# Attention on Trainium2: queries and keys projected as channels by tokens, rotated there, and stacked per head by way of DRAM

## The chip, the core and the metric

One core of a Trainium2 chip runs the whole network, in one launch. The metric is the time on the device of one execution, in microseconds (us): 2022.48 us before the change, the median of 3 runs (2022.04 to 2023.08).

The engines are TensorE (PE; the loading of its stationary operand is shown apart, as PEld), VectorE (DVE), ScalarE (ACT), GpSimd (POOL) and SyncE (SP), which here only issues DMAs. SBUF is the memory on the chip, with 128 partitions; TensorE writes to PSUM; DRAM is reached by DMA. 1024 tokens, 1024 channels, all in float32. A large product is done as three products of split operands (`mm3`): hi x hi, hi x lo and lo x hi, where hi is the value rounded to the type float32r and lo the rest.

## The reference

Two layers: attention, then an HGRN recurrence, each followed by an MLP. The change lies in the attention of the first layer.

```python
def sliding_window_attention(h, positions, w_qkv, b_qkv, sinks, w_o):
    qkv = h @ w_qkv + b_qkv                      # 1024 tokens, 16 query heads, 4 key and value heads, 64 channels a head
    q, k, v = ...
    cos, sin = rotary_tables(positions)
    q = apply_partial_rotary(q, cos, sin)        # rotates the first 16 of the 64 channels: pairs (i, i + 8)
    k = apply_partial_rotary(k, cos, sin)
    # blocks of 128 tokens, each with its own and the previous block as keys
    scores = einsum('bnqkgd,bnskd->bnkgqs', qb, kb) * HEAD_DIM ** -0.5
    scores = where(mask, scores, NEG_INF)        # causal, window of 128
    m = maximum(max(scores), sink); e = exp(scores - m)
    probs = e / (sum(e) + exp(sink - m))
    return einsum('bnkgqs,bnskd->bnqkgd', probs, vb).reshape(...) @ w_o
```

h is the input after an rmsnorm with a gain. The kernel multiplies by the gain first and by the token's factor 1/rms after the projection.

## The kernel before

**Order of the work.** The program first writes all operations into a list (`Schedule.add`), each with the engine or engines it may run on, a planned cost and what it reads and writes. `Schedule.order` then plays the list forward with the planned costs and latencies (a DMA load 4.2 us, a store 3.2 us), taking on each engine the ready operation of the lowest rank, and back for due times; the best of four such passes gives the order in which each engine's instructions are issued and the buffer of each tile. On the chip that order is fixed: each engine works through its own list, and an instruction that waits holds those behind it. SP's list holds all large DMAs, so a load that must wait for a store holds the weight loads behind it. Tiles come from pools of fixed size, `BUFS`: 60 "a" tiles and 18 "t" tiles of 128x512, 6 raw weight tiles "wr", 5 each of split ones "wh" and "wl", 8 PSUM banks ("p" and "q", 4 each).

**Attention.** Tokens go in two halves of 512 (four blocks of 128). `attention` runs `qkv(0)` alone, then `attend(0)` between `qkv(1)`, then `attend(1)` between `o_proj(0)`, then `o_proj(1)` between the first pieces of the MLP.

`qkv` has three groups of 512 columns: `cg` 0 holds keys and values (256 each), 1 and 2 the queries of two pairs of key heads. Each group runs over 8 slices of the input channels (`kt`), with one weight tile each, and four blocks: tokens are the stationary operand, the weights move, and PSUM holds 128 tokens by 512 columns. 12 products of 512 columns to a weight tile, 96 to a group.

`projected` takes a block of queries out of PSUM on VectorE (factor and bias in one operation) and rotates it there: tokens lie in the partitions, so the tables `trig` are 128x8 for a block, and a rotation is four small operations (`rope`). `keys_values` does the same for keys, turns them into channels by tokens with two transposes on TensorE, and fills for each of three overlapping spans of blocks (`K_SPANS`) the tiles `ks` (hi, in both halves of the partitions; the second copy is made by POOL) and `kl` (lo in one half, zero in the other).

`attend` turns the queries the same way, 16 transposes for each pair of key heads and half, and writes `stacks`: a tile for each head with hi in 64 partitions and lo in the other 64. The scores of a block are then two products a head, of the stack with `ks` and with `kl`. After them come the masks, the softmax (with the sink as one more column), transposes of the probabilities and the products with the values.

Of the kernel before, what the change touches and what calls it, by code (L numbers as in the profile page):

```python
# [10 lines left out]
F32 = mybir.dt.float32  # L11
# [6 lines left out]
P = 128  # L18
# [3 lines left out]
NH = 2  # L22
# [19 lines left out]
CH = 64  # L42
QB = 32
LEVELS = 5
HOMES = "aaaaaaaaaaaa"
K_SPANS = ((-1, 3), (2, 6), (5, 8))

# [36 lines left out]
class Buf:  # L84
# [7 lines left out]
    def keys(self, part):  # L92
        return set(self.writer) | set(self.readers) if part is None else {*part, None}
# [287 lines left out]
class Net:  # L381
# [751 lines left out]


    def rope_tables(self):
        shape = (P, NBLK, ROT // 2)
        pos = self.const((P, NBLK), I32)
        self.dma(pos, self.io["pos"], 4 * P * NBLK)
        posf = self.const((P, NBLK))
        self.op("DVE", self.nc.vector.tensor_copy, [posf], [pos], 100, posf, pos)  # L1140
        ang = self.const(shape)
        for j, f in enumerate(INV_FREQ):
            self.ts("DVE", ang[:, :, j], posf, f, None, ALU.mult, None, NBLK)
        self.trig = []
        for shift in (0.25, 0.0):
            turns, r = self.const(shape), self.const(shape)
            n = NBLK * ROT // 2
# [9 lines left out]
            self.trig.append(r)  # L1157

    def attention_constants(self):
# [3 lines left out]
        self.bias = []  # L1163
        for cg in range(3):
            b = self.a()
            self.dma(b, self.io["bqkv"][cg].partition_broadcast(P), 4 * P * TH)
            self.bias.append(b)
# [9 lines left out]
    def rope(self, x, heads, n):  # L1177
        half = ROT // 2
        v = x.rearrange("p (h d) -> p h d", d=HD)[:, :, :ROT].rearrange("p h (a r) -> p h a r", a=2)
        prod = []  # L1180
        for tab in self.trig:
            y = self.t(F32, (P, 8, 2, half))[:, :heads]
            tb = tab[:, n].unsqueeze(1).unsqueeze(1).to_broadcast([P, heads, 2, half])
            self.tt("any", y, v, tb, ALU.mult, heads * ROT)
            prod.append(y)
        yc, ys = prod
        self.tt("any", v[:, :, 0], yc[:, :, 0], ys[:, :, 1], ALU.subtract, heads * half)
        self.tt("any", v[:, :, 1], yc[:, :, 1], ys[:, :, 0], ALU.add, heads * half)

    def k_tiles(self, i):  # L1190
        if self.ks[i] is None:
            late = [] if i else [self.x[KT - 1][0]]
            self.ks[i] = [self.a(F32R) for _ in range(NG)]
            self.kl[i] = [self.t(F32R) for _ in range(NG)]
            for g, z in enumerate(self.kl[i]):
                _, o = self.rows(g)
                self.memset(z[o].bitcast(F32).only("o"), 0.0, "Pool", late)
            if K_SPANS[i][0] < 0:
                for z in self.ks[i] + self.kl[i]:
                    self.memset(z[:, :P].bitcast(F32).only(-1), 0.0, "Pool", late)  # L1200
        return self.ks[i], self.kl[i]

    def rows(self, g):
        lo, hi = slice(0, HD), slice(HD, P)
        return (hi, lo) if g % 2 else (lo, hi)

    def first_loads(self):

# [16 lines left out]

    def qkv(self, hf, h, r, ahead=()):

        blocks = range(hf * BPH, hf * BPH + BPH)
        for cg in range(3):
            ps = {n: self.psum() for n in blocks}  # L1230
            for kt in range(KT):
                self.s.lead = LEAD
                c = kt % 2 * TH
# [3 lines left out]
                w = self.weight_split(raw, engines=("DVE", "ACT") if start else ("ACT",), parts=start)  # L1237
                self.s.lead = 0
                hh, hl = h[kt]
                for n in blocks:  # L1240
                    tok = slice((n % BPH) * P, (n % BPH) * P + P)
                    hi = hh[:, tok].only(n // 2) if start else hh[:, tok]
                    self.mm3(ps[n], (hi, hl[:, tok]), w, kt == 0, kt == KT - 1)
                    if kt == KT - 1:
                        self.projected(cg, n, ps[n], r[:, n % BPH : n % BPH + 1])
                yield

    def projected(self, cg, n, ps, r):
        if cg == 0:
            self.keys_values(n, ps, r)  # L1250
        else:
            q = self.a()
            self.stt(q, ps, r, self.bias[cg], ALU.mult, ALU.add)
            self.rope(q, 8, n)
            self.q[n][cg - 1] = q

    def keys_values(self, n, ps, r):
        W = NG * HD
        k = self.t(F32, (P, W))
        self.stt(k, ps[:, :W], r, self.bias[0][:, :W], ALU.mult, ALU.add, W)  # L1260
        if n % 2 == 0:
            self.v.append(self.a(F32, (P, 2, W)))
        v = self.v[n // 2][:, n % 2].only(n)
        self.stt(v, ps[:, W:], r, self.bias[0][:, W:], ALU.mult, ALU.add, W)
# [5 lines left out]
        self.rope(k, NG, n)  # L1270
        pk = self.psum("q")[:, : 2 * P].rearrange("p (g s) -> p g s", g=2)
        for gp in range(2):
            self.transpose(pk[:, gp], k[:, gp * P : gp * P + P])
        for i, (first, end) in enumerate(K_SPANS):
            if not first <= n < end:
                continue
            ks, kl = self.k_tiles(i)
            c = slice((n - first) * P, (n - first) * P + P)
            for g in range(NG):
                r, o = self.rows(g)  # L1280
                src, dst = pk[r, g // 2], ks[g][r, c].only(n)
                self.copy(dst, src, P, more=HALF["ACT"])
                self.tt("DVE", kl[g][r, c].only(n), src, dst.bitcast(F32), ALU.subtract, P, HALF["DVE"])
                self.ts("Pool", ks[g][o, c].only(n), dst, 1.0, None, ALU.mult, None, P)

    def attend(self, hf, out):

        blocks = range(hf * BPH, hf * BPH + BPH)
        for gp in range(NG // 2):
            stacks = [[None] * 4 for _ in range(2)]  # L1290
            for j in range(4):
                pq = self.psum("q")
                for n in blocks:
                    c = slice((n % BPH) * P, (n % BPH) * P + P)
                    self.transpose(pq[:, c], self.q[n][gp][:, j * P : j * P + P])
                for e in range(2):
                    r, o = self.rows(e)
                    s = self.a(F32R)
                    self.act(s[r], pq[r], AF.Copy, scale=HD**-0.5, more=HALF["ACT"])
                    self.stt(s[o], pq[r], HD**-0.5, s[r].bitcast(F32), ALU.mult, ALU.subtract, more=HALF["DVE"])  # L1300
                    stacks[e][j] = s
            for e in range(2):
                g = 2 * gp + e
                for j in range(2):
# [75 lines left out]

    def attention(self, layer):
        self.v, self.dv, self.ks, self.kl = [], [], [None] * 3, [None] * 3
        self.q = [[None] * 2 for _ in range(NBLK)]
        out = [{}, {}]
        ahead = self.first_loads()
        h = [self.scaled(layer, 0)]
# [548 lines left out]
def layout(i):  # L1935
# [8 lines left out]
    heads = np.arange(D).reshape(2, 2, 4, HD).transpose(0, 2, 1, 3).ravel()  # L1944
    cols = np.concatenate([np.arange(D, D + 2 * NG * HD), heads])
    rows = [
        (4 * g + 2 * r + j) * HD + d for g in range(NG) for j in range(2) for r in range(2) for d in range(HD)
    ]
# [5 lines left out]
        "pos": f(i["positions"][0].reshape(NBLK, P).T),  # L1954
        "sinks": f(i["attn_sinks"][0]),
        "bqkv": f(bq[cols].reshape(3, TH)),
# [44 lines left out]
```

## Time and profile before

| | |
|---|---|
| median of 3 runs | 2022.48 us |
| profiled execution, its own time | 2021.7 us |
| its span | 2019.9 us |
| granted TensorE clock | 0.999 of full |
| TensorE busy | 2009.3 us (99%) |
| VectorE busy | 1844.6 us (91%) |
| ScalarE busy | 1312.5 us (65%) |
| POOL busy | 61.7 us (3%) |
| bytes read and written in DRAM | 394.57 MB, 100.14 MB |

Names in the profile are the program's, without numbers: `a<-q` is an operation that reads a PSUM tile "q" and writes an "a" tile, `d` is a tile in DRAM, `c` a constant. In a row of a group stand the shapes, the count, the busy time in us, the mean duration of one in ns, the engine's idle time just before them in us, and what ended it. In the timeline a row has the start, the length in us, engine, line, operation, names, shapes and how many instructions were merged. Nearly every operation is recorded by the same helper, so all rows have line 435. Ends of matmuls are modelled, so the time of one is longer than its step in a run of them.

### The profile page before, as it was taken

What the parts mean: (1) busy time and instruction counts of PE and PEld (TensorE: products, weight loads), DVE (VectorE), ACT (ScalarE), POOL (GpSimd) and SP (SyncE); (2) the same over time, 40 slices, a digit from 0 to 9 for tenths busy, and PEclk for the clock granted to TensorE, in tenths of its full rate; (3) what the DMA queues carried; (4) which work ended last, traced back from release to release, by engine and by line L of the source; (5) the groups of instructions that cost most, each with busy time, mean ns of one, the idle gap of its engine ahead of it and who ended that gap; (6) DMA issues with size and microseconds to landing.
All of it is one profiled execution on the core that took longest, in us unless ns stands there. A gap on an engine that the chain in (4) does not pass through costs nothing.

```text
span 2019.9 us, 39908 instructions
## 1 busy us (share of the span) xinstructions
PE 2009.3 (99%) x13788; PEld 1702.1 (84%) x13788; DVE 1844.6 (91%) x3802; ACT 1312.5 (65%) x2775; POOL 61.7 (3%) x152
## 2 busy tenths in 40 slices
PE   9999999999999999999999999999999999999998
PEld 7878788899998888888888888888889998888887
DVE  8899989899999979989999999999999999997985
ACT  7577977667676544657666666676767677544573
POOL 4020000000000000000000000000000000000000
PEclk9999999999999999999999999999999999999999
DMA  6212487778889987845878889999798888997812
GB/s 230 79 48 74 136 260 259 257 253 284 282 272 316 319 280 234 272 162 185 284 280 285 288 284 317 316 303 315 260 296 288 267 294 284 325 316 235 270 53 84
DMA packets 275418, 497.38 MB, mean 246 GB/s; under 512 B 30992, under 2 KB 36368, under 8 KB 275216
## 3 DMA queue, kind: packets, MB, share of 16 engines
q1 hardware_dynamic: 275072, 494.81, 73.1%
q8 instruction: 109, 1.79, 0.4%
q14 instruction: 93, 0.76, 0.1%
q10 hardware_dynamic: 144, 0.02, 0.0%
HBM read 394.57 MB, written 100.14 MB: 245 GB/s over the span
## 4 chain that ended last, share of the span: by engine, by line
PE 91%; DVE 6%; ACT 1%; issue 1%; DMA 1%; SPq 0%; DVEq 0%; ACTq 0%
PE p L435 50%; PE q L435 41%; DVE t L435 2%; DVE a L435 1%; DVE m L435 1%; DVE wl L435 1%; DMA a<-d 0%; ACT a L435 0%; ACT t L435 0%; SPq L435 0%; ACT wh L435 0%; DVE sm L435 0%; DMA a<-in_x 0%; ACT m L435 0%; DVEq L1975 0%
## 5 line engine op out<-in xcount | busy, mean ns | idle before, releaser
L435 PE MATMUL p<-a,wh 128*128 128x512 f32 (+1 forms) x2832 | 779.7, 360 | 0.0
L435 PE MATMUL q<-a,wh 128*128 128x512 f32 x2020 | 624.6, 390 | 0.2 <-ACT t L435 0.2
L435 PEld LDWEIGHTS p<-a,wh 128*128 128x128 f32 x2832 | 502.1, 189 | 78.4 <-issue 0.4
L435 PE MATMUL p<-a,wl 128*128 128x512 f32 (+1 forms) x1416 | 504.5, 359 | 0.6 <-DVE wl L435 0.6
L435 PEld LDWEIGHTS q<-a,wh 128*128 128x128 f32 x2020 | 374.8, 188 | 74.2 <-ACT t L435 0.6
L435 PE MATMUL q<-a,wl 128*128 128x512 f32 x1008 | 391.3, 389 | 0.0
L435 ACT CAST wh<-m 128x512 fp32r<-128x512 f32 (+1 forms) x354 | 212.0, 605 | 208.7 <-PE q L435 100.9
L435 PEld LDWEIGHTS p<-a,wl 128*128 128x128 f32 x1416 | 266.0, 189 | 39.2 <-DVE wl L435 1.4
L435 ACT CAST wh<-wr 128x512 fp32r<-128x512 f32 (+1 forms) x324 | 194.4, 603 | 154.4 <-PE p L435 92.6
L435 DVE TENSOR_TENSOR wl<-m,wh 128x512 fp32r<-128x512 f32 (+1 forms) x354 | 235.4, 670 | 35.0 <-ACT wh L435 28.8
L435 DVE TENSOR_TENSOR wl<-wr,wh 128x512 fp32r<-128x512 f32 (+1 forms) x324 | 215.0, 668 | 20.9 <-ACT wh L435 19.7
L435 DVE TENSOR_TENSOR t<-t,t 128x512 f32<-128x512 f32 (+4 forms) x408 | 225.1, 576 | 7.2 <-ACT t L435 4.4
L435 DVE TENSOR_TENSOR a<-t,a 128x512 fp32r<-128x512 f32 (+2 forms) x321 | 211.1, 677 | 16.8 <-PE q L435 7.1
L435 PEld LDWEIGHTS q<-a,wl 128*128 128x128 f32 x1008 | 189.3, 188 | 39.2
L435 ACT ACTIVATE t<-t 128x512 f32<-128x512 f32 x288 | 179.1, 631 | 53.2 <-DVE t L435 47.1
L435 ACT CAST a<-t 128x512 fp32r<-128x512 f32 (+1 forms) x241 | 142.8, 606 | 24.3 <-DVE t L435 9.2
L435 ACT COPY t<-q 128x512 f32<-128x512 f32 (+2 forms) x254 | 111.3, 442 | 32.1 <-PE q L435 23.0
L435 DVE TENSOR_TENSOR t<-t,p 128x256 f32<-128x256 f32 x288 | 116.4, 417 | 15.9 <-PE p L435 11.9
L435 PE MATMUL p<-wh,a 128*128 128x512 f32 x384 | 124.7, 395 | 0.2
L435 DVE TENSOR_TENSOR m<-wr,wr 128x512 f32<-128x512 f32 (+1 forms) x184 | 119.7, 652 | 0.4
L435 DVE TENSOR_TENSOR a<-a,a 128x512 fp32r<-128x512 f32 (+2 forms) x151 | 100.8, 682 | 8.4 <-ACT a L435 4.7
L435 ACT CAST a<-a 128x512 fp32r<-128x512 f32 x136 | 82.5, 620 | 26.7 <-DVE a L435 21.1
(131 smaller groups left out, 2434.2 us busy)
## 6 DMA issues: line engine op xcount, KB each, us to landing
t<-d SPq DMA_DIRECT2D x592, 256.0 KB, 4.6
a<-d SPq DMA_DIRECT2D x318, 256.0 KB, 4.6
d<-t SPq DMA_DIRECT2D x290, 256.0 KB, 3.3
wr<-in_down SPq DMA_DIRECT2D x224, 256.0 KB, 4.2
wr<-in_up SPq DMA_DIRECT2D x172, 256.0 KB, 4.3
wr<-in_win SPq DMA_DIRECT2D x68, 256.0 KB, 5.2
d<-a SPq DMA_DIRECT2D x64, 256.0 KB, 3.4
wr<-in_wqkv SPq DMA_DIRECT2D x48, 256.0 KB, 2.8
```

The lines of the kernel that those rows point to most:

```text
L435: fn(*[place(a) for a in args], **{k: place(v) for k, v in kw.items()})
```

## The change

Queries and keys are now projected with the weights as the stationary operand and the 512 tokens of a half moving: PSUM holds 128 channels by 512 tokens. Values stay as they were, now as products of 256 columns. Columns of the weights are ordered so that the first of a group's tiles holds the rotated channels of its heads: the first of each pair in the upper 64 partitions, the second in the lower; the others hold channels that aren't rotated.

- `channels` multiplies by the token factor, spread over partitions (`shares`, from four products of 128x128 for each half), adds the bias (now one value to a partition) on ScalarE, and splits into hi and lo. A rotated tile is also copied with its halves exchanged (`other`, two ScalarE operations of 64 partitions) and combined with two tables on VectorE.
- `rope_tables` computes the angles in 128x64 (8 frequencies by 16 pieces of 64 tokens) and keeps cos, sin and -sin in DRAM; `table` loads each into 128x512 tiles by DMAs that repeat the 8 rows, once for keys and once for queries in each half.
- `rows_out` stores hi and lo in DRAM, in the order in which the heads need them: `dk` for keys, `dq` for each half and pair.
- `keys` loads `ks` and `kl` of each span from `dk`: `ks` by a source with a leading dimension of 2 and step 0. `kl` has its lo in the lower partitions' half for all heads.
- `attend` loads its 8 stacks of a pair from `dq`. All transposes of queries and keys are gone, and so are the three 128x512 bias tiles; the order of the coroutines and the pools are unchanged.

```diff
+    def table(self, hf, keys):
+        cos, sin = self.a(), self.a()
+        half, h = P // 2, ROT // 2
+        n = 2 * NG * h // 2 if keys else half
...
+        for z, k, d in ((cos, 0, 0), (cos, half, 0), (sin, 0, 2), (sin, half, 1)):
+            src = self.trig[d].rearrange("(i c) t -> i (c t)", i=h)[:, hf * TH : hf * TH + TH]
+            self.dma(z[k : k + n].only(k), src.unsqueeze(0).to_broadcast([n // h, h, TH]), 4 * n * TH)
+        return cos, sin
...
+    def channels(self, ps, r, bias, tables=None):
+        z, hi, lo = self.t(), self.t(F32R), self.t(F32R)
+        self.tt("DVE", z, ps, r, ALU.mult)
+        if tables is None:
+            self.act(hi, z, AF.Identity, bias=bias)
+            self.stt(lo, z, bias, hi.bitcast(F32), ALU.add, ALU.subtract)
+            return hi, lo
+        y, other = self.t(), self.t()
+        up, low = slice(0, P // 2), slice(P // 2, P)
+        self.act(y, z, AF.Identity, bias=bias)
+        for i, (a, b) in enumerate(((up, low), (low, up))):
+            self.act(other[b].only(i), z[a], AF.Identity, bias=bias[a], more=HALF["ACT"])
+        cos, sin = tables
+        self.tt("DVE", y, y, cos, ALU.mult)
+        self.tt("DVE", other, other, sin, ALU.mult)
+        self.tt("DVE", y, y, other, ALU.add)
+        self.copy(hi, y, TH, psum=False)
+        self.tt("DVE", lo, y, hi.bitcast(F32), ALU.subtract)
+        return hi, lo
+
+    def keys(self, hf, ps, r, tables):
+        q = P // 4
+        first = [(slice(i * q, i * q + q), d) for i, d in enumerate((0, ROT, ROT // 2, 3 * ROT // 2))]
+        bias = [self.bias[:, i : i + 1] for i in range(2)]
+        self.rows_out(self.dk, NG, self.channels(ps[0], r, bias[0], tables), first, hf)
+        self.rows_out(self.dk, NG, self.channels(ps[1], r, bias[1]), [(slice(0, P), 2 * ROT)], hf)
...
+        rows = self.dk.rearrange("(g s d) t -> g s d t", g=NG, s=2)
+        for i, (first, end) in enumerate(K_SPANS):
+            a, b = max(first, hf * BPH), min(end, hf * BPH + BPH)
...
+            for g in range(NG):
+                src = [rows[g, s][:, a * P : b * P].only(*read(s)) for s in range(2)]
+                self.dma(ks[g][:, c].bitcast(F32).only(*range(a, b)), src[0].unsqueeze(0).to_broadcast([2, HD, n]), 4 * P * n)
+                self.dma(kl[g][:HD, c].bitcast(F32).only(*range(a, b)), src[1], 4 * HD * n)
+
+    def rows_out(self, d, heads, parts, pieces, hf=None):
+        for s, z in enumerate(parts):
+            for rows, first in pieces:
+                n = rows.stop - rows.start
+                to = d.rearrange("(h s d) t -> h s d t", h=heads, s=2)[:, s, first : first + n // heads]
...
+                self.dma(to.only(...), z[rows].bitcast(F32), 4 * n * TH)
+
+    def queries(self, hf, gp, m, ps, r, tables):
+        half = P // 2
+        bias = self.bias[:, 2 + 4 * gp + m : 3 + 4 * gp + m]
+        parts = self.channels(ps, r, bias, None if m else tables)
+        pieces = [(slice(0, P), ROT * m)] if m else [(slice(0, half), 0), (slice(half, P), ROT // 2)]
+        self.rows_out(self.dq[hf, gp], NHQ // 2, parts, pieces)
...
     def qkv(self, hf, h, r, ahead=()):
-        blocks = range(hf * BPH, hf * BPH + BPH)
+        W = NG * HD
+        shares, tables = [self.a() for _ in range(2)], None
         for cg in range(3):
-            ps = {n: self.psum() for n in blocks}
+            if cg == 0:
+                kp, vp = ([self.psum() for _ in range(2)] for _ in range(2))
+            else:
+                qp = [self.psum() for _ in range(4)]
...
+                for b in range(BPH if cg == 0 else 0):
+                    tok = slice(b * P, b * P + P)
+                    hi = hh[:, tok].only(b // 2) if start else hh[:, tok]
+                    self.mm3(vp[b // 2][:, b % 2 * W : b % 2 * W + W], (hi, hl[:, tok]), tuple(z[:, W:] for z in w), ...)
+                for m, ps in enumerate(qp if cg else kp):
+                    self.mm3(ps, tuple(z[:, m * P : m * P + P] for z in w), (hh, hl), first, last)
                 yield
...
+            if cg == 0:
+                total = self.spread(r)
+                for z, scale in zip(shares, (1.0, HD**-0.5)):
+                    self.act(z, total, AF.Copy, scale=scale)
+                self.keys(hf, kp, shares[0], self.table(hf, True))
+                for b in range(BPH):
+                    self.value(hf * BPH + b, vp[b // 2][:, b % 2 * W : b % 2 * W + W], r[:, b : b + 1])
+                tables = self.table(hf, False)
+            else:
+                for m, ps in enumerate(qp):
+                    self.queries(hf, cg - 1, m, ps, shares[1], tables)
...
     def attend(self, hf, out):
         for gp in range(NG // 2):
-            stacks = [[None] * 4 for _ in range(2)]
-            for j in range(4):
-                pq = self.psum("q")
-                for n in blocks:
-                    c = slice((n % BPH) * P, (n % BPH) * P + P)
-                    self.transpose(pq[:, c], self.q[n][gp][:, j * P : j * P + P])
...
+            stacks = [[self.a(F32R) for _ in range(4)] for _ in range(2)]
+            for k, z in enumerate(sum(stacks, [])):
+                self.dma(z.bitcast(F32), self.dq[hf, gp][k * P : k * P + P], 4 * P * TH)
```

More of the change, by code (lines that the diff above doesn't have):

```diff
@@ L1157, in rope_tables @@
             self.trig.append(r)
+        minus = self.const((P, n))
+        self.ts("DVE", minus, self.trig[1], -1.0, None, ALU.mult, None, n)
+        kept = []
+        for z in (self.trig[0], self.trig[1], minus):
+            d = self.tile(f"d{self.n}", 1, (P, n), F32, self.dram)
+            self.dma(d, z, 4 * P * n)
+            kept.append(d)
+        self.trig = kept
+    def table(self, hf, keys):
+        cos, sin = self.a(), self.a()
+        half, h = P // 2, ROT // 2
+        n = 2 * NG * h // 2 if keys else half
+        if keys:
+            for k in (n, half + n):
+                self.memset(cos[k : k + n].only(f"o{k}"), 1.0, "Pool")
+                self.memset(sin[k : k + n].only(f"o{k}"), 0.0, "Pool")
+        for z, k, d in ((cos, 0, 0), (cos, half, 0), (sin, 0, 2), (sin, half, 1)):
+            src = self.trig[d].rearrange("(i c) t -> i (c t)", i=h)[:, hf * TH : hf * TH + TH]
+            self.dma(z[k : k + n].only(k), src.unsqueeze(0).to_broadcast([n // h, h, TH]), 4 * n * TH)
+        return cos, sin
     def attention_constants(self):
@@ L1162, in attention_constants @@
         self.dma(self.sink, self.io["sinks"].partition_broadcast(P), 4 * P * NHQ)
[L1163 to L1167, printed above, removed]
+        W = NG * HD
+        self.bias_v, self.bias = self.const((P, W)), self.const((P, 10))
+        self.dma(self.bias_v, self.io["bv"].partition_broadcast(P), 4 * P * W)
+        self.dma(self.bias, self.io["bqk"], 4 * P * 10)
+        self.ts("DVE", self.bias[:, 2:], self.bias[:, 2:], HD**-0.5, None, ALU.mult, None, 8)
         diff = self.t(I32, (P, P))
@@ L1175, in attention_constants @@
         self.memset(self.neg, NEG)
[L1177 to L1188, printed above, removed]
+        self.dk = self.tile(f"d{self.n}", 1, (2 * NG * HD, T), F32, self.dram)
@@ new lines, in attention_constants @@
+        self.dq = {(hf, gp): self.tile(f"d{self.n}", 1, (NHQ * HD, TH), F32, self.dram) for hf in range(NH) for gp in range(2)}
+    def channels(self, ps, r, bias, tables=None):
[17 more added lines that the diff above has]
+        return hi, lo
@@ new lines, in rows_out @@
+    def rows_out(self, d, heads, parts, pieces, hf=None):
[3 more added lines that the diff above has]
+                to = d.rearrange("(h s d) t -> h s d t", h=heads, s=2)[:, s, first : first + n // heads]
+                if hf is not None:
+                    to = to[:, :, hf * TH : hf * TH + TH]
+                self.dma(to.only(f"{'' if hf is None else hf}{s}{first}"), z[rows].bitcast(F32), 4 * n * TH)
+    def queries(self, hf, gp, m, ps, r, tables):
[4 more added lines that the diff above has]
+        self.rows_out(self.dq[hf, gp], NHQ // 2, parts, pieces)
@@ L1194, in k_tiles @@
             self.kl[i] = [self.t(F32R) for _ in range(NG)]
-            for g, z in enumerate(self.kl[i]):
-                _, o = self.rows(g)
-                self.memset(z[o].bitcast(F32).only("o"), 0.0, "Pool", late)
+            for z in self.kl[i]:
+                self.memset(z[HD:].bitcast(F32).only("o"), 0.0, "Pool", late)
             if K_SPANS[i][0] < 0:
-                for z in self.ks[i] + self.kl[i]:
+                for z in self.ks[i]:
                     self.memset(z[:, :P].bitcast(F32).only(-1), 0.0, "Pool", late)
+                for z in self.kl[i]:
+                    self.memset(z[:HD, :P].bitcast(F32).only(-1), 0.0, "Pool", late)
         return self.ks[i], self.kl[i]
-    def rows(self, g):
-        lo, hi = slice(0, HD), slice(HD, P)
-        return (hi, lo) if g % 2 else (lo, hi)
     def first_loads(self):
@@ L1239, in qkv, with value @@
                 hh, hl = h[kt]
-                for n in blocks:
[L1241 to L1245, printed above, removed]
-                yield
[L1248 to L1257, printed above, removed]
+                first, last = kt == 0, kt == KT - 1
+                for b in range(BPH if cg == 0 else 0):
+                    tok = slice(b * P, b * P + P)
+                    hi = hh[:, tok].only(b // 2) if start else hh[:, tok]
+                    self.mm3(vp[b // 2][:, b % 2 * W : b % 2 * W + W], (hi, hl[:, tok]), tuple(z[:, W:] for z in w), first and b % 2 == 0,
+                             last, W, skip_group_check=True)
+                for m, ps in enumerate(qp if cg else kp):
+                    self.mm3(ps, tuple(z[:, m * P : m * P + P] for z in w), (hh, hl), first, last)
+                yield
+            if cg == 0:
[9 more added lines that the diff above has]
+                    self.queries(hf, cg - 1, m, ps, shares[1], tables)
+    def value(self, n, ps, r):
         W = NG * HD
-        k = self.t(F32, (P, W))
-        self.stt(k, ps[:, :W], r, self.bias[0][:, :W], ALU.mult, ALU.add, W)
         if n % 2 == 0:
@@ L1269, in keys_values @@
             self.tt("any", self.dv[n // 2][:, n % 2].only(n), v, before, ALU.subtract, W)
[L1270 to L1284, printed above, removed]
     def attend(self, hf, out):
@@ L1943, in layout @@
     bq, wq = i["attn_b_qkv"][0], i["attn_w_qkv"][0]
-    heads = np.arange(D).reshape(2, 2, 4, HD).transpose(0, 2, 1, 3).ravel()
-    cols = np.concatenate([np.arange(D, D + 2 * NG * HD), heads])
+    head = lambda first, n, *dims: np.concatenate([np.add.outer(first + HD * np.arange(n), np.arange(*d)).ravel() for d in dims])
+    h = ROT // 2
+    keys = head(D, NG, (0, h), (ROT, ROT + h), (h, ROT), (ROT + h, 2 * ROT), (2 * ROT, HD))
+    queries = [head(gp * D // 2, NHQ // 2, (0, h), (h, ROT), *((k, k + ROT) for k in range(ROT, HD, ROT))) for gp in range(2)]
+    cols = np.concatenate([keys, np.arange(D + NG * HD, D + 2 * NG * HD), *queries])
     rows = [
@@ L1953, in layout @@
         "lb": f(col(lb)),
[L1954 removed]
+        "pos": f(np.broadcast_to(i["positions"][0].reshape(1, NCH, T // NCH), (ROT // 2, NCH, T // NCH)).reshape(P, T // NCH)),
         "sinks": f(i["attn_sinks"][0]),
[L1956 removed]
+        "bqk": f(bq[np.concatenate([keys, *queries])].reshape(10, P).T),
+        "bv": f(bq[D + NG * HD : D + 2 * NG * HD]),
         "wqkv": f(wq[:, cols].reshape(4, 2, P, 3, TH).transpose(3, 0, 2, 1, 4).reshape(3, 4, P, 2 * TH)),
```

40 lines of the change are left out of this document (22 added, 18 removed).

## The prediction

> **What bounds the kernel now.** I read the first part of the page (busy time of each engine), then the chain that ended last, then busy time in stretches of 25 us over the attention stage.
>
> ```profile
> span 2019.9 us, 39908 instructions
> PE 2009.3 (99%) x13788; PEld 1702.1 (84%) x13788; DVE 1844.6 (91%) x3802; ACT 1312.5 (65%) x2775; POOL 61.7 (3%) x152
> PE 91%; DVE 6%; ACT 1%; issue 1%; DMA 1%; SPq 0%; DVEq 0%; ACTq 0%
> 25.00:50.00 25.00, 25.00 (x116) 20.66 (x115) 23.95 (x65) 19.45 (x47) 14.72 (x24) 1.00 0.52 164
> 50.00:75.00 25.00, 25.00 (x151) 20.77 (x149) 19.64 (x55) 8.40 (x14) 2.10 (x4) 1.00 0.28 86
> 75.00:100.00 25.00, 25.00 (x137) 21.05 (x136) 23.63 (x61) 20.45 (x61) 1.96 (x6) 1.00 0.24 75
> 100.00:125.00 25.00, 24.79 (x145) 19.62 (x145) 21.17 (x66) 19.64 (x72) 10.63 (x21) 1.00 0.06 22
> ```
>
> The columns of a stretch are its length, then PE, PEld, DVE, ACT and POOL busy, the granted clock, the DMA share and GB/s. TensorE is the bound in every stretch and at full clock; VectorE is close behind it in the attention stage; the DMA engines are the only ones with room there. So a us of TensorE work taken out is a us gained, work on ScalarE, VectorE or POOL is worth almost nothing, and whatever makes TensorE wait is paid in full.
>
> **TensorE's own work.** The change takes out 80 transposes: 64 of queries (2 halves x 2 pairs of groups x 4 x 4 blocks) and 16 of keys. It adds two spreads of the norm factors over the partitions, 4 products of 128x128 each. The projections keep their count in columns; only the values' go from 512 columns to 256 (192 products instead of 96).
>
> ```profile
> L435 PE MATMUL q<-c,a 128*128 128x128 f32 x64 | 8.7, 274 | 0.0
> L435 PE MATMUL q<-c,t 128*128 128x128 f32 x16 | 2.8, 274 | 0.2 <-ACT a L435 0.2
> 73.25 1.97 PE L435 MATMUL q<-c,a 128*128 128x128 f32 x16
> L435 PE MATMUL q<-c,sm 128*128 128x128 f32 x32 | 4.4, 279 | 1.0 <-DVE sm L435 1.0
> 116.04 0.40 PE L435 MATMUL q<-a,a 128*128 128x256 f32 x2
> 116.27 0.40 PE L435 MATMUL q<-t,a 128*128 128x256 f32 x2
> 116.51 0.63 PE L435 MATMUL p<-wh,a 128*128 128x512 f32 x2
> 116.98 0.39 PE L435 MATMUL p<-wl,a 128*128 128x512 f32 x1
> 117.21 0.63 PE L435 MATMUL p<-wh,a 128*128 128x512 f32 x2
> ```
>
> The groups give 8.7 + 2.8 = 11.5 us, but the drain of the last product of each run is in that. Sixteen in a row took 1.97 us, 0.123 each: 80 x 0.123 = 9.8, the value I take. Spreads of the same form (two rows of the trace to a product) cost 4.4/32 = 0.14 a row, 16 rows: +2.2. Four products of 256 columns start within 0.47 us (0.1175 each), three of 512 within 0.70 (0.233): two short ones cost at most 0.005 more than a long one, 96 x 0.005 = +0.5. Sum on TensorE: -9.8 + 2.2 + 0.5 = **-7.1 us** (between -9.0 with 11.5 and -6).
>
> **ScalarE, VectorE and POOL.**
>
> ```profile
> L435 DVE SCALAR_TENSOR_TENSOR a<-q,a 64x512 fp32r<-64x512 f32 x32 | 21.8, 688 | 0.7
> L435 DVE TENSOR_TENSOR t<-q,a 64x128 fp32r<-64x128 f32 x40 | 11.5, 288 | 0.7
> L435 DVE SCALAR_TENSOR_TENSOR a<-p,sm,a 128x512 f32<-128x512 f32 x16 | 11.4, 744 | 2.0 <-PE p L435 2.0
> L435 DVE TENSOR_TENSOR t<-a,c 128x128 f32<-128x128 f32 x32 | 8.0, 282 | 0.0
> L435 DVE TENSOR_TENSOR a<-t,t 128x64 f32<-128x64 f32 x32 | 5.7, 218 | 0.1
> L435 DVE TENSOR_TENSOR a<-p,t 128x512 f32<-128x512 f32 x13 | 8.9, 686 | 3.1 <-PE p L435 3.0
> L435 ACT ACTIVATE a<-q 64x512 fp32r<-64x512 f32 x32 | 18.4, 590 | 0.5
> L435 ACT CAST a<-q 64x128 fp32r<-64x128 f32 x40 | 10.4, 260 | 3.0 <-PE q L435 2.0
> L435 ACT ACTIVATE a<-a,c 128x512 fp32r<-128x512 f32 x15 | 10.6, 716 | 0.5 <-DMA a<-in_x 0.5
> L435 POOL TENSOR_SCALAR a<-a 64x128 fp32r<-64x128 f32 x40 | 24.4, 611 | 8.6 <-ACT a L435 6.1
> ```
>
> VectorE loses the five first rows, 58 us, and some small ones of the keys. It gains, over 20 channel tiles (2 of keys and 8 of queries in each half), a product with the norm factor (20 x 0.69), a remainder with bias in 14 (0.74) and four operations of 0.69 in the 6 that are rotated: 13.8 + 10.4 + 16.6 = 41 us. Net about -17, and it is no bound. ScalarE loses 28.8 and gains 14 x 0.72 for the tiles that are not rotated, some 2.6 for each of the 6 rotated ones, and 4 copies of the spread factors at 0.6: 28 us; even. POOL loses 24.4. All of this lies beside TensorE. The angles' small operations at the start are about as many as before, and the tables that come of them are due only when the first keys are rotated.
>
> **The DMAs, the term that decides.** Before, keys and queries stayed in SBUF. Now each half writes 4 tiles of keys (hi and lo of two channel tiles) and 16 of queries, reads 16 stacks of 256 KB back, and reads each key span twice (`ks`, the high part doubled over 128 rows, 1.31 MB a half, and `kl`). All go through SP's one queue, among the weights, and what is issued behind other transfers lands later (below: the x tiles of the opening burst 5.4 us, weights 2.8). SP issues in order: a load that waits for a store's landing holds all weight loads behind it.
>
> ```profile
> q1 hardware_dynamic: 275072, 494.81, 73.1%
> wr<-in_wqkv SPq DMA_DIRECT2D x48, 256.0 KB, 2.8
> a<-in_x SPq DMA_DIRECT2D x15, 256.0 KB, 5.4
> d<-t SPq DMA_DIRECT2D x11, 256.0 KB, 4.1
> t<-d SPq DMA_DIRECT2D x8, 256.0 KB, 4.8
> 30.36 0.39 PE L435 MATMUL q<-c,t 128*128 128x128 f32 x2
> 78.19 0.36 PE L435 MATMUL q<-a,a 128*128 128x256 f32 x1
> 107.51 0.38 PE L435 MATMUL q<-c,t 128*128 128x128 f32 x2
> 180.82 0.60 PE L435 MATMUL q<-c,a 128*128 128x128 f32 x4
> ```
>
> First column after the names: count, size, us from issue to landing. The near bound: every transfer spreads over all 16 engines as these 256 KB ones do. Then the queries of the first pair of groups, whose projection ends one group of 96 products (96 x 0.23 = 22 us) after the first keys at 30.4, are out of the arithmetic at about 58, stored by 62 (4.1) and back by 70 (4.8 and a few behind each other), 8 us before the first scores at 78.19. All is hidden, cost 0, and the weights are held up for a few us at most, against a lead of 6 raw and 5 split tiles of 12 products each, 11 x 12 x 0.23 = 30 us.
>
> The far bound: a transfer is dealt to the engines by its outermost dimension. Every large transfer in the trace has 128 rows outermost. The new ones do not: `ks` reads a source written as 2 copies of 64 rows, the stores of the keys run over 4 heads, those of the queries over 8. Dealt so, `ks` runs on 2 engines, the others on 4 and 8, and the lowest engines carry all of them in turn. One engine needs 0.731 x 16 x 2019.9 / 494.81 = 48 us for a MB. On the busiest engine, from the first keys ready at about 38 (30.4, spread and scaling, then five steps of 0.7 behind the tables): stores of keys 1.05 MB/4, 12.5 us, landed at 52; then `ks` 1.31 MB/2, 31.3, `kl` 2.0 and six weight tiles 4.7, to 90; the queries' stores, issued at 56 to 62 but behind these, 2.1 MB/8, 12.5, to 102; four stacks 3.1 and a landing of 2.8, to 108. The first scores wait from 78 to 108: **30 us**, with SP held at the stack loads, the weights behind it, and the hi and lo tiles of the queries (8 of 18 buffers "t") not free until their stores land, so VectorE cannot read the next projections from PSUM either. In the second half the same chain of 70 us starts 8 us after the keys at 107.5 and ends at 185.5; its first scores follow the transposes at 180.82: 4 us more. Sum 34 us.
>
> The Trainium skill has this case in "DMA: Bandwidth & Descriptors", section "Rules for kernel authors": an outermost dimension of fewer than 16, such as a leading zero-stride broadcast of c copies, confines the whole DMA to at most c engines. By that rule the sum is the far one, without it the near one; no run here shows either yet.
>
> I take the far bound. No row has such a pattern, so the nearest rows, all of 128 outermost, speak neither way; what I go by is that 128 rows falling into 16 engines evenly is what dealing by rows gives, and that a dealing that ignored the pattern would have to cut a strided source at places that the instruction does not name. The sum: 2021.7 (the profiled execution's own time) + 34 - 7.1 = 2048.6; the median of the runs shown is 0.8 above that execution, so **2049 us**.
>
> **Rivals.** *Spread over all engines, hidden:* 2022.5 - 7.1 = 2015 us. For it: a DMA share of 0.06 to 0.28 between 50 and 125, and new traffic of some 24 MB that 16 engines move in 24 x 48/16 = 72 us. Against: the patterns. It decides if the chain from keys to stacks takes under 40 us instead of 70, that is if `ks` and the stores take 30 us less on their busiest engine. This is the case that ends on the other side.
>
> *A partial stall that eats the gain:* the order of work is planned ahead, and the plan may hold second-half projections between the end of the first half and the first scores. Each weight tile there is 2.8 us of cover; with 8 of them the 30 us shrink to 8, the gain is used up, about 2023. Against it: the planner takes ready work in program order, and by its own latencies the stacks are there in time, so it has no reason to put other work first.
>
> *Too few "t" tiles, whatever the engines do:* 12 of 18 can be held by key remainders, up to 8 by blocks whose values are not done, and now a channel group needs 14 (5 + 3 x 3), each kept for about 6 us (three steps of 0.7 and a store's 4.1). With 4 free, 14 x 6/4 = 21 us per group, of which TensorE covers some 15 with other products; at three groups of the second half that is 3 x 6 = 18 us, 2022.5 - 7 + 18 = 2033. For it: VectorE is already 23.6 of 25 us busy there; against: groups in the first half meet no attention work.
>
> **Numbers.** Few engines, with stalls: 0.62 (own range 2030 to 2072, from a stall of 15 to one where both halves wait 30). "t" tiles: 0.08. Partial stall: 0.10, split as 0.08 within 0.2% and 0.02 faster. All hidden: 0.20, faster. What a measurement of this kernel can tell from no change is about 0.2%, 4 us. So slower 0.70, same 0.08, faster 0.22. Cases of both signs hold weight, so the range runs from the hidden case's 2014 to 2072; below lies half of the hidden case's spread, above the worst stalls.
>
> **What the profile after would show.** The rows `q<-c,a` and `q<-c,t` of 128 columns gone, and TensorE's work outside its gaps shorter by 7 us, confirm the gain. The landing of the `ks` loads decides: near 5 us means spread, far above 10 us means few engines. Then TensorE should idle between about 78 and 108, with the DMA of a stack (`a<-d`) as releaser, weight loads issued late in the same stretch, and the share of busy DMA engines low while it waits. If `ks` lands fast and TensorE has no gap there, the forecast is wrong and 2015 is right; if the gap is there but the releaser is a VectorE operation on "t" tiles, the third rival was.

## The result, and the profile after

The changed kernel takes 2070.66 us (median of 5 runs, 2068.91 to 2071.66), the kernel before in the same comparison 2022.07: a ratio of 1.0238, 95% interval 1.0223 to 1.0253. It is slower by 48.6 us; 2049, that is 27 us slower, was forecast.

The first part of the page after, with what moved (`q1` is the queue that SP fills):

```profile
span 2069.9 us, 40061 instructions
PE 2015.2 (97%) x13820; PEld 1709.1 (83%) x13820; DVE 1820.3 (88%) x3680; ACT 1310.8 (63%) x2745; POOL 40.3 (2%) x121
q1 hardware_dynamic: 289712, 518.67, 75.0%
```

VectorE lost 24 us of work, POOL 21, ScalarE 2; none of it shows in the time. TensorE's busy time rose although it has less to do, because its products ran at a lower clock for a while. The stretches of 25 us show where (length, PE, PEld, DVE, ACT and POOL busy, granted clock, DMA share, GB/s):

```profile
50.00:75.00 25.00, 18.98 (x84) 15.39 (x82) 7.45 (x12) 5.57 (x9) 0.00 (x0) 0.97 0.40 128
75.00:100.00 25.00, 10.99 (x31) 7.68 (x32) 8.79 (x15) 7.33 (x13) 0.00 (x0) 0.64 0.61 194
100.00:125.00 25.00, 19.69 (x139) 17.89 (x139) 13.60 (x27) 14.68 (x38) 1.26 (x3) 0.84 0.56 193
...
175.00:200.00 25.00, 13.64 (x79) 11.52 (x77) 10.92 (x21) 11.48 (x37) 0.45 (x2) 0.86 0.30 96
200.00:225.00 25.00, 19.01 (x98) 14.93 (x99) 15.92 (x29) 12.83 (x40) 0.67 (x3) 0.80 0.64 194
```

Two holes, one after the projections of each half. No engine is near full in these stretches, and the DMA engines are busy for 0.30 to 0.64 of the time only. That fits work that waits for transfers which do not use all of them; the experiments test it. TensorE's own timeline, the lines with a long idle time before them (in brackets, with what ended it):

```profile
81.37 1.22 PE L436 MATMUL p<-a,wh 128*128 128x512 f32 x2 [12.39 <-ACT wh L436]
96.58 1.20 PE L436 MATMUL q<-a,a 128*128 128x256 f32 x2 [6.34 <-issue]
...
116.18 0.63 PE L436 MATMUL q<-c,m 128*128 128x128 f32 x4 [2.55 <-DVE m L436]
121.29 0.79 PE L436 MATMUL q<-a,a 128*128 128x256 f32 x2 [2.76 <-DVE t L436]
162.44 0.63 PE L436 MATMUL q<-c,m 128*128 128x128 f32 x4 [1.19 <-DVE m L436]
205.99 1.22 PE L436 MATMUL p<-a,wh 128*128 128x512 f32 x2 [17.35 <-DVE t L436]
```

These and two shorter ones, 0.41 and 0.73, make 43.7 us. The releasers named are ScalarE and VectorE; the waits of the first 330 us (total, times, longest) say what those two waited for, stores that had not landed and so did not free their "t" tiles:

```profile
ACT t L436 <- DMA d<-t: 41.2, 5, 23.1
DVE t L436 <- ACT t L436: 36.0, 12, 22.9
DVE t L436 <- DMA d<-t: 19.4, 4, 17.0
PE p L436 <- DVE t L436: 18.4, 2, 17.4
```

So a store holds a tile, ScalarE or VectorE waits for the tile, the projection's PSUM tile is not read, and TensorE waits for that.

### The profile page after: what moved, and what is told of

The parts are those of the page before. It is cut to its first block, busy times and chain, and to the rows that moved or that the text cites. A ratio compares the mean times of both kernels' runs of the same rounds, so it can differ in the third digit from the quotient of the medians.

```text
span 2069.9 us, 40061 instructions
## 1 busy us (share of the span) xinstructions
PE 2015.2 (97%) x13820; PEld 1709.1 (83%) x13820; DVE 1820.3 (88%) x3680; ACT 1310.8 (63%) x2745; POOL 40.3 (2%) x121
## 5 line engine op out<-in xcount | busy, mean ns | idle before, releaser
L436 PE MATMUL p<-a,wh 128*128 128x512 f32 (+1 forms) x3152 | 884.9, 365 | 29.9 <-DVE t L436 17.5
L436 PEld LDWEIGHTS p<-a,wh 128*128 128x128 f32 x3152 | 562.4, 190 | 120.0 <-DVE t L436 18.1
L436 PE MATMUL p<-a,wl 128*128 128x512 f32 (+1 forms) x1576 | 568.8, 363 | 0.7 <-DVE wl L436 0.7
L436 PEld LDWEIGHTS p<-a,wl 128*128 128x128 f32 x1576 | 297.2, 190 | 46.6 <-DVE wl L436 1.9
L436 DVE TENSOR_TENSOR t<-t,t 128x512 f32<-128x512 f32 (+3 forms) x404 | 229.3, 593 | 36.9 <-ACT t L436 33.9
L436 PE MATMUL p<-t,wh 128*128 128x256 f32 x480 | 90.7, 283 | 0.0
```

Source lines behind the costliest of these rows:

```text
L436: fn(*[place(a) for a in args], **{k: place(v) for k, v in kw.items()})
```

## The experiments

**Is it how the transfers fall on the engines?** `e1_ks_two` loads each `ks` by two transfers of 64 rows:

```diff
-                self.dma(ks[g][:, c].bitcast(F32).only(*range(a, b)), src[0].unsqueeze(0).to_broadcast([2, HD, n]), 4 * P * n)
+                for half in range(2):
+                    to = ks[g][half * HD : half * HD + HD, c].bitcast(F32).only(*(f"{half}{k}" for k in range(a, b)))
+                    self.dma(to, src[0], 4 * HD * n)
...
```

The lines left out only name the two halves of a `ks` tile separately, where it is cleared and where the scores read it.

> Edit: each `ks` tile is loaded by two transfers of 64 rows in place of one whose source has a leading dimension of 2; the same bytes, 16 more transfers in all. Few engines: the 31 us that `ks` takes on its two engines become 1.31 MB/16, 4 us, in each half; the chain from the first keys to the stacks shrinks from 70 to about 43 us, and the stores over 4 and 8 heads remain: 2018 to 2035 us, with a gap of at most some 10 us left. Too few "t" tiles: the tiles' number and life inside the half are the same but for the stores' landing, so at least two thirds of the loss stays: above 2050. If a DMA spreads over the engines whatever its pattern: no change, 2070.

Measured: 2040.93 us, 1.0093 of before (1.0078 to 1.0109); 29.7 us below the changed kernel, with the same bytes and 16 transfers more. That is 6 us above the expected 2018 to 2035, and 9 below the 2050 of the other theory.

`e2_rows` leaves `ks` as it is and reorders columns and rows, so that the stores and the loads of the rotation tables have channels outermost (only the changed parts of the lines are shown):

```diff
-to = d.rearrange("(h s d) t -> h s d t", h=heads, s=2)[:, s, first : first + n // heads]
+to = d.rearrange("(h s d) t -> h s d t", h=heads, s=2)[:, s, first : first + n // heads].rearrange("h d t -> d h t")
-src.unsqueeze(0).to_broadcast([n // h, h, TH])
+src.unsqueeze(1).to_broadcast([h, n // h, TH])
-np.add.outer(first + HD * np.arange(n), np.arange(*d)).ravel() for d in dims
+np.add.outer(np.arange(*d), first + HD * np.arange(n)).ravel() for d in dims
```

> Edit: the columns of the weights and the table rows are ordered channel by channel instead of head by head, so that the stores of keys and queries and the table loads run over 8 to 32 channels outermost instead of 4 and 8 heads; `ks` stays as it is, the same number of transfers. Few engines: key stores fall from 12.5 to 4.7 us and query stores from 12.5 to 7.9 on the busiest engine, `ks` keeps its 31 us: the chain shrinks by 12 of 70 us in each half: 2045 to 2062. Too few "t" tiles: the stores land sooner, a gain of at most a few us: 2062 to 2070.

Measured: 2052.21 us, 1.015 (1.0133 to 1.0167); 18.5 us below the changed kernel, as the few engines have it.

`e3_both` makes both edits.

> Edit: both of the above, two transfers of 64 rows for each `ks` and channels outermost in the stores. Few engines: the whole chain is hidden, TensorE has no gap over 2 us after the first 25 us, and only its 7 us less work are left: 2012 to 2020. Too few "t" tiles: above 2040.

Measured: 2022.91 us, 1.0003 (0.9994 to 1.0012). That is 3 us above the expected 2012 to 2020, and one gap of more than 2 us is left (2.91, below). 47.8 us are gone; the two edits alone gave 29.7 + 18.5 = 48.2. The long idle times of TensorE's timeline, first `e1_ks_two`, then `e2_rows`, then `e3_both`:

```profile
84.50 1.87 PE L436 MATMUL q<-a,a 128*128 128x256 f32 x3 [9.33 <-issue]
...
175.79 1.22 PE L436 MATMUL p<-a,wh 128*128 128x512 f32 x2 [3.07 <-DVE t L436]
```

```profile
73.34 1.22 PE L436 MATMUL p<-a,wh 128*128 128x512 f32 x2 [4.35 <-ACT wh L436]
...
183.92 1.22 PE L436 MATMUL p<-a,wh 128*128 128x512 f32 x2 [14.41 <-DVE t L436]
```

```profile
91.49 0.63 PE L436 MATMUL q<-c,m 128*128 128x128 f32 x4 [2.91 <-DVE m L436]
94.63 0.50 PE L436 MATMUL q<-a,a 128*128 128x256 f32 x2 [1.10 <-DVE t L436]
157.54 0.73 PE L436 MATMUL p<-a,wh 128*128 128x512 f32 x2 [0.32 <-DVE t L436]
```

`ks` made most of the second half's gap: 17.35 us fall to 3.07 without it and to 14.41 with it alone. The first half's idle time falls from 25.2 us to 13.2 and 10.8 under one edit, and to 4.6 only under both. This settles the main cause: the same bytes cost 48 us or nothing according to the outermost dimension of their patterns. The rule of the Trainium skill that the prediction cited ("DMA: Bandwidth & Descriptors", "Rules for kernel authors") agrees with these three runs.

The landing of the `ks` loads, which the prediction named as the sign that decides, can't be read: for the changed kernel the profile gives no times from issue to landing. The share of busy DMA engines, the last column but one, answers in its place. In the changed kernel it stands still at certain steps:

```profile
44.00:47.00 3.00, 3.00 (x15) 2.49 (x14) 0.69 (x1) 0.62 (x1) 0.00 (x0) 1.00 0.27 103
70.00:72.00 2.00, 0.00 (x0) 0.00 (x0) 0.00 (x0) 0.00 (x0) 0.00 (x0) 1.00 0.13 46
80.50:83.50 3.00, 1.72 (x3) 1.00 (x4) 2.60 (x5) 1.86 (x4) 0.00 (x0) 0.50 0.53 186
```

Of 16 engines, 4 busy ones are a share of 0.25, 2 are 0.125 and 8 are 0.5. Of the 170 stretches of 1 us from 30 to 200 us, 25 show a share of 0.11 to 0.15 in the changed kernel, 22 in `e2_rows`, which keeps its `ks`, none in `e1_ks_two` and 1 in `e3_both`. A share of 0.24 to 0.28 shows in 19, 3, 17 and 6 of them, in the same order: it goes with the stores and table loads over 4 heads. The share reads a little high, above 1 in places, and it does not name the engines, but the steps, and the edits that remove them, are those of 2 and 4 engines.

**Is it the number of "t" tiles?** `e4_tiles` keeps the transfers and writes the lo part over the scaled tile:

```diff
-        z, hi, lo = self.t(), self.t(F32R), self.t(F32R)
+        z, hi = self.t(), self.t(F32R)
+        lo = z.bitcast(F32R)
...
-        y, other = self.t(), self.t()
+        y, other = z, self.t()
```

with the operation that makes `y` moved behind those that make `other`.

> Edit: the changed kernel with its transfers as they are, but the lo part written in place over the scaled tile, and the rotated tile too: 2 "t" tiles for a plain channel tile instead of 3, 3 instead of 5 for a rotated one, so 9 instead of 14 for a group. Few engines: the stores and `ks` take as long as before and the first scores still wait for the stacks: 2055 to 2072. Too few "t" tiles: the stall falls by half or more: below 2045.

Measured: 2062.68 us, 1.0201 (1.0186 to 1.0216). With 9 tiles instead of 14, 8 us are gained and 40 stay. Its timeline shows the wait that was there behind the tiles, the scores waiting for a stack (`a<-d`):

```profile
96.21 0.55 PE L436 MATMUL q<-a,a 128*128 128x256 f32 x1 [20.57 <-DMA a<-d]
...
199.77 0.79 PE L436 MATMUL p<-a,wh 128*128 128x512 f32 x1 [13.98 <-DVE t L436]
```

So tiles are one way by which the wait reaches TensorE in the changed kernel, not why it is there.

**Would a plan that knows the delay cover it?** `e10_plan` is the changed kernel with only the planner's latency of the stores raised from 3.2 to 23.2 us.

> Edit: the changed kernel with all its transfers as they are (2, 4 and 8 engines), and only the planner told that stores of keys and queries land after 23.2 us instead of 3.2. If the loss is there because the fixed order put the scores where the plan thought the stacks to be, other work now covers part of it: 2030 to 2058. If the waits can't be covered (no other work, "t" tiles held as long): 2060 to 2075.

Measured: 2099.35 us, 1.0379 (1.0365 to 1.0393), 29 us worse than the changed kernel and above both expectations. The scores still wait for a stack, and later, at 130 us; the second gap grows too:

```profile
129.86 0.55 PE L436 MATMUL q<-a,a 128*128 128x256 f32 x1 [23.19 <-DMA a<-d]
...
228.13 1.22 PE L436 MATMUL p<-a,wh 128*128 128x512 f32 x2 [22.85 <-DVE t L436]
```

The later plan covered neither gap. Why it came out worse, and whether another delay, or one for `ks` too, would have covered part of the wait, was not tried.

**Where are the 7 us that TensorE no longer works?** `e3_both` has them, and is not faster. Its stretches against those of before show TensorE idle in two places, at the start (22.60 us busy against 23.70) and at the first attention blocks (20.54 against 25.00). First the opening stretch of before, then the two of `e3_both`:

```profile
0.00:25.00 25.00, 23.70 (x132) 18.87 (x133) 20.05 (x60) 20.04 (x33) 6.03 (x22) 1.00 0.89 301
```

```profile
0.00:25.00 25.00, 22.60 (x165) 20.52 (x166) 21.99 (x70) 19.45 (x34) 12.06 (x37) 1.00 0.87 278
...
75.00:100.00 25.00, 20.54 (x169) 18.70 (x170) 17.66 (x36) 18.79 (x52) 1.49 (x4) 1.00 0.74 236
```

That is 1.1 + 4.5 = 5.6 us more of idle time in an equal span. Five runs went after it. `e5_merge` is `e3_both` with one store of 128 rows for the rotated query tile in place of two of 64:

```diff
-    pieces = [(slice(0, P), ROT * m)] if m else [(slice(0, half), 0), (slice(half, P), ROT // 2)]
+    pieces = [(slice(0, P), ROT * m)]
```

> Edit: e3_both, and the rotated query tile stored by one transfer of 128 rows for each part instead of two of 64 (8 transfers fewer in all, that run on 16 engines instead of 8). What is left of the loss in e3_both is ScalarE at 80 to 83 us waiting 3.7 us for a store (`d<-t`) to free a "t" tile, then VectorE waiting for ScalarE 5.8, then TensorE for VectorE 2.9 and 1.1. If that is a matter of when the stores land: 1 to 3 us gained, 2019.5 to 2022. If it is a matter of how many "t" tiles there are: 2021 to 2024, as e3_both.

Measured: 2021.43 us, 0.9994 (0.9986 to 1.0003), inside both expectations, so it does not choose between them, and no different from before. `e6_all` adds the reuse of the scaled tile as in `e4_tiles`.

> Edit: e5_merge, and the scaled tile reused for the rest (9 "t" tiles for a group of queries instead of 14). Too few "t" tiles as what is left of the loss: the waits of ScalarE for a store and of TensorE at 88 to 95 us go, and the 7 us less work of TensorE show, less about 1 us of a later start: 2015 to 2019. If the residue is stores that land late, or a mistake in the 7 us: 2020 to 2024.

Measured: 2020.94 us, 0.9993 (0.9984 to 1.0002). This is the second expectation: the tiles are not what is left of the loss here. ScalarE still waited for a store, 4.29 us where it was 3.7 in `e3_both`:

```profile
84.24 1.25 ACT L436 ACTIVATE t<-a 128x512 f32<-128x512 f32 x2 [4.29 <-DMA d<-t]
```

`e7_first` moves the first weight tile's load ahead of the first input tile's in the program.

```diff
             x = self.x[kt][0] = self.a()
+            if kt == 0:
+                ahead.append(self.raw(self.io["wqkv"][0, 0][:, :TH]))
...
-            if kt < BUFS["wr"]:
+            if 0 < kt < BUFS["wr"]:
```

> Edit: e6_all, and the first weight tile's load put ahead of the first input tile's in the program, as the load order of the kernel before had it. The first product of the projections started at 6.4 us in the changed kernel, 4.6 before, and TensorE was 1 us of work behind at 20 us: 0.5 to 1.5 us below e6_all. If the start is set by something else (the split of that tile on two engines): as e6_all within 0.5.

Measured: 2018.94 us, 0.9983 (0.9974 to 0.9992), 2.0 below `e6_all` where 0.5 to 1.5 were expected: the best of all, 3 us below before. The first product of the projections starts at 4.92 us in place of 6.11. That is 1.2 us; the rest must come from elsewhere, since another plan was drawn as well: at 75 to 100 us TensorE is busy for 22.77 us at a clock of 1.00, against 21.57 at 0.93 in `e6_all`.

`e8_late` tells the planner of `e7_first` that the stores land after 8.2 us and the stacks after 6.2, and `e9_late_wide` does so without the reuse of the tile.

> Edit: e7_first, with the planner told a later landing: 8.2 us instead of 3.2 for the stores of keys and queries, 6.2 instead of 4.2 for the stacks. Nothing else. What is left of the loss in e7_first and e6_all is ScalarE at 80 us waiting 2.8 to 4.3 us for a store to free a "t" tile. If that is the plan's error about when stores land: the wait goes and some 2 to 3 us are gained, 2015 to 2017. If there are too few tiles however it is planned: the plan shows the wait as idle time in another place, 2018 to 2021.

> Edit: e8_late without the reuse of the scaled tile, so 14 "t" tiles for a group again. If the number of tiles costs anything once the plan knows the landing: 2 us or more above e8_late. If not: within 1 us of it.

Measured: 2019.26 us, 0.9985 (0.9976 to 0.9994), and 2024.08 us, 1.001 (1.0001 to 1.0019). `e8_late` gained nothing over `e7_first`, as its second expectation had it: ScalarE's wait for a store there is nearly gone, but it now waits for scores instead:

```profile
81.50 0.37 ACT L436 COPY m<-q 128x256 f32<-128x256 f32 x1 [1.43 <-PE q L436]
82.20 0.62 ACT L436 CAST wh<-wr 128x512 fp32r<-128x512 f32 x1 [0.32 <-DMA d<-t]
```

`e9_late_wide` is 4.8 us slower than `e8_late`, with a gap for "t" tiles in the second half, so the 14 tiles do seem to cost something once the plan keeps them longer; another plan was drawn here too:

```profile
158.27 0.72 PE L436 MATMUL p<-a,wh 128*128 128x512 f32 x2 [3.55 <-DVE t L436]
```

So 3 of the 7 us were had; how much of the rest can be had at all stays open.

## Why the prediction was right, and where it was off

**The bound and what decides.** TensorE bounds the kernel, and only its waits counted: 46 us of work taken off VectorE and POOL together brought nothing, while transfers on few engines cost 48 us. The far bound was the right one to take; `e3_both`, its condition taken away, lands within 0.1% of before. The size was short: 48.6 us slower against 27 forecast, and 2070.66 lies just inside the range that ended at 2072. That it still lies inside owes something to luck, because the second half's wait and the clock, below, were not foreseen. One reading at the start was too strong, without effect on the sum: the DMA engines were not the only ones with room, as ScalarE was busy for 8.40 us of the 25 from 50 to 75, and POOL for 2.10.

**-7.1 us of TensorE's work.** `e3_both` measures it, with modelled ends as before and at the same granted clock (0.999):

```profile
PE 2003.6 (99%) x13820; PEld 1700.9 (84%) x13820; DVE 1819.9 (90%) x3680; ACT 1310.5 (65%) x2745; POOL 40.7 (2%) x121
```

That is 5.7 us less than the 2009.3 of before, just short of the forecast's 6 to 9. The rows `q<-c,a` and `q<-c,t` of 128 columns are gone, as foretold. The work fell, but the span did not, since TensorE idles as much longer.

**30 us in the first half.** The mechanism was right, the place and the releaser only in part. The gap was foretold from 78 to 108, for a stack. It began at 69, for "t" tiles that the stores held, which the prediction named but priced as lying beside the wait for the stacks. The sign that it had set, a stack's load or a VectorE operation on "t" tiles as what ends the gap, gave neither here: ScalarE's `wh` ended it, behind a wait of 23.1 us for a store. In the second half it pointed to the third rival. It could not tell the two apart, because slow stores are what holds the tiles. With fewer tiles held (`e4_tiles`) the scores waited for a stack from 75.6 to 96.2. So the chain of transfers ended 12 us earlier there than the ledger's 108. Its price of 48 us for a MB on one engine was too dear: the steps above are 103 GB/s on four engines and 46 on two, that is 39 and 43 us for a MB. At 41 the ledger's 66 us on the busiest engine become 56, by estimate 10 of the 12. TensorE's idle times up to 125 us add to 25.2 us, against 30.

**4 us in the second half.** This term failed: 18.5 us of idle time were measured (17.35 + 1.19). The step took the second half's chain to matter only at the first scores at 180.82. What stopped TensorE there was the other effect, VectorE waiting 17.0 us for a store to free a tile, with the last projections unread in PSUM, and `e1_ks_two` shows that `ks` on few engines was what kept those stores.

**The clock.** The prediction left it out. After the longer gaps TensorE runs at half of its clock for some us. In stretches of 3 us of the changed kernel, before, in and after the first gap:

```profile
57.00:60.00 3.00, 3.00 (x15) 2.46 (x14) 0.90 (x2) 0.06 (x1) 0.00 (x0) 1.00 0.53 159
...
69.00:72.00 3.00, 0.00 (x0) 0.00 (x0) 0.00 (x0) 0.00 (x0) 0.00 (x0) 1.00 0.27 81
72.00:75.00 3.00, 0.00 (x0) 0.00 (x0) 0.00 (x0) 0.00 (x0) 0.00 (x0) 0.76 0.51 143
75.00:78.00 3.00, 0.00 (x0) 0.00 (x0) 0.00 (x0) 0.00 (x0) 0.00 (x0) 0.50 0.30 112
...
84.00:87.00 3.00, 3.00 (x8) 2.30 (x7) 0.15 (x1) 0.00 (x0) 0.00 (x0) 0.50 0.49 154
87.00:90.00 3.00, 3.00 (x14) 2.35 (x12) 0.00 (x0) 0.00 (x0) 0.00 (x0) 0.97 0.71 201
```

The clock falls between 72 and 75, some 4.6 us into the gap, and is back at 87, nearly 6 us after work began again at 81.4; meanwhile 8 products pass in 3 us instead of 15. There are four such spells: work began again at 81.4, 96.6, 121.3 and 206.0 us, and by such stretches the clock was back at about 87.2, 104.3, 128.2 and 210.1. Half of the time TensorE worked in them is lost, 2.9 + 3.5 + 3.4 + 2.1, an estimate of 12 us. The third spell followed two short gaps, of 2.55 and 2.76 us:

```profile
123.00:126.00 3.00, 3.00 (x42) 2.57 (x42) 2.02 (x6) 2.48 (x12) 0.00 (x0) 0.50 0.39 99
126.00:129.00 3.00, 3.00 (x15) 2.61 (x14) 2.74 (x5) 2.68 (x9) 0.00 (x0) 0.64 0.45 148
```

The gap of 3.07 us in `e1_ks_two` brought the clock down too (first two lines), the one of 2.91 in `e3_both` did not (last line):

```profile
173.00:176.00 3.00, 0.21 (x1) 0.22 (x2) 0.96 (x2) 0.00 (x0) 0.00 (x0) 0.87 0.70 162
176.00:179.00 3.00, 3.00 (x10) 2.47 (x11) 2.57 (x6) 2.14 (x8) 0.34 (x1) 0.56 0.57 195
...
90.00:93.00 3.00, 1.51 (x11) 1.42 (x11) 2.83 (x5) 3.00 (x7) 0.84 (x2) 1.00 0.57 207
```

The Trainium skill says in "TensorE: Matmul & The Clock Gate", part 1, that the clock halves after at least one idle window of about 3.4 us and comes back after a busy one. The long gaps agree; the two spells after shorter gaps show that here less than 3.4 us of unbroken idleness was enough. The sum against `e3_both`, whose span is 50.0 us shorter: idle times of 43.7 - 4.9 (the three shown for `e3_both` and one of 0.60) = 38.8, and 12 for the clock, 50.8.

**The rivals.** *All engines, hidden* was wrong for this kernel, and right for `e3_both` but for the gain, which the first attention blocks ate. *Partial stall* was wrong: the plan covered too little to eat the gain, and told of a later landing it did worse (`e10_plan`). *"t" tiles* alone don't explain the loss (`e3_both` has 14 of them a group and no loss), but they carry it: 8 us of 48 in `e4_tiles`, and perhaps the 4.8 of `e9_late_wide` against `e8_late`.

## What to carry to other kernels

Read the outermost dimension of every DMA pattern before reading its bytes: a broadcast written as (2, 64, n) or a store written as (heads, channels, n) can leave most DMA engines idle, and two transfers of 64 rows and reordered weight columns mended it here. A share of busy DMA engines that stands still at 2/16, 4/16 or 8/16 is the sign to look for. Where a load waits for a store, price what the store still holds, tiles and the queue behind it, and not only the consumer of the load. A gap of TensorE costs its length and, where it brought the clock down in the changed kernel, 2 to 3.5 us more, by the estimate above; gaps of about 3 us went either way.

## What the runs showed of the hardware beyond that

SP took longer over some of its DMA issues in the changed kernel. Issue times in ns (min, median, max) of the loads and stores through DRAM in the first 250 us, the changed kernel and then `e3_both`:

```profile
L436 SPq DMA_DIRECT2D d<-t x58: 531/583/4532, 33.9 to 250.0; - x58
...
L436 SPq DMA_DIRECT2D t<-d x16: 489/1396/3840, 55.9 to 191.4; - x16
```

```profile
L436 SPq DMA_DIRECT2D d<-t x61: 327/574/1227, 33.9 to 228.6; - x61
L436 SPq DMA_DIRECT2D t<-d x16: 444/594/1097, 48.6 to 148.0; - x16
```

An issue took up to 4.5 us in the one and 1.2 in the other. A likely reason is that busy DMA engines held the issue up; the trace does not show it. If so, transfers on few engines hold not only what waits for them but also the one queue through which weights come, a second way to cost time that the prediction did not have. How much of the 48 us went that way was not tried apart.
